# One Hymba decoder layer: the order of work inside a Mamba-2 chunk group, and the place of two small gate bounds

## The chip, the cores and the metric

The kernel runs on one core of one Trainium2 chip, as a single launch. The metric is the device time of a launch in microseconds (us); smaller is better. One core has a matrix engine (PE), a vector engine (DVE), a scalar engine (ACT), a general engine (POOL) and an engine that mostly issues transfers (SP). Each engine works through its own queue strictly in order, and semaphores make an instruction wait for work of another engine or for a transfer.

## The reference

One inference step of a hybrid decoder layer for a prompt of 1024 tokens (with 16 learned tokens ahead of it, so 1040) and 8 single-token samples, width 1024. In outline:

```python
h = h + 0.5 * swiglu(rmsnorm(h, n1), w1g, w1u, w1d)          # FFN1
u = rmsnorm(h, nm) @ w_in                                    # one input projection
# HGRN2 heads: lb comes from lb_logits alone
lb = cumsum(softmax(lb_logits, axis=0), axis=0)[layer]
f = lb + (1 - lb) * sigmoid(u_f) ...
# Mamba-2 heads, chunk by chunk (128 tokens):
def step(h, inp):
    xc, dtc, bc, cc = inp
    cum = cumsum(dtc * a_g, axis=1)
    seg = exp(where(causal, cum_t - cum_s, -inf))
    cb  = einsum('btgn,bsgn->bgts', cc, bc)
    y   = einsum('bgts,bgrts,bsgr,bsgrp->btgrp', cb, seg, dtc, xc)
    y   = y + einsum('btgn,bgrpn,btgr->btgrp', cc, h, exp(cum))
    h   = h * exp(last) + einsum('bsgn,bsgr,bgrpn...', bc, dtc * exp(last - cum), xc)
    return h, y
h = h + concat(hgrn_out, ssm_out) @ w_out
h = h + 0.5 * swiglu(rmsnorm(h, n2), w2g, w2u, w2d)          # FFN2
```

All inputs and outputs are f32.

## The kernel before, in words

The layer is written as one program: FFN1, the input projection, the Mamba-2 scan, the HGRN2 heads, the output projection, FFN2. Large products are made of three matmuls each, on operands split in a high and a low part (`mm3`, L173 to L175). The order of the instructions on PE is the order of the code; on the other engines a scheduler sets it when the program is built, from the code's order and its own due times, and it is fixed from then on.

The Mamba-2 scan (`ssm_scan`, L1610) runs over nine chunks c, eight of 128 tokens and one of 16. `front(c)` prepares a chunk, `back(c, hT)` makes its output and the next state. One **group** of the scan is `back(c)`, `front(c + 2)` and then `fill(10)`, ten steps of the input projections of later heads, of three matmuls each, which give PE work while the other engines prepare the next group. What the letters stand for:

- `mt`, the decay mask of a chunk for 8 heads (128 x 1024). SP issues its transfer (L1622, 512 KB, from `cumd`), ACT makes it with eight relu instructions (L1649) and one exp (L1650), and DVE multiplies it with `cbm`, the masked B-C products (L1644), in two instructions (L1652). It takes the buffer that the mask of chunk c-2 had.
- `xdt` (L1638), `xw` (L1653): the inputs scaled, on DVE, from `px`, a transpose on PE (L1633). `xw` is split: `xh` on ACT (L167), `xl` on DVE (L168).
- `bt`: the transposed B (PE L1641 into `pb`, where L1643 puts the B-C products too), its high part cast on ACT (L1645), its low part on DVE (L1646).
- `pi`: PE's product of state and C (L1667), read by DVE L1668. `py`: PE's product of `xdt` and `mt` (L1672), read by the add DVE L1675. Then four L1688 write the outputs.
- `ps`: PE's state product of `bt`, `xh`, `xl` (twelve matmuls on tiles `t`). The new state hn is the old one times a decay (DVE L1684) plus `ps` (DVE L1685). The next `pi` needs hn.

px, pb, pi, py and ps share four PSUM banks (tag `mis`) in rotation, in the order in which the code asks for them: in a group of the kernel before pi, py, ps, px, pb. So pb stands five places behind pi and gets the bank that pi had in the same group.

`constants_mix` (L1256) prepares small constants between FFN1 and the projections. Its seven small DVE instructions L1285 to L1294 and one ACT exp (L1288) make `lb` and `oml`, the bounds of the HGRN2 gates. `after1` places single steps into the second half of FFN1 by the number of a step (`S.before(e3 + ..., ...)`).

Of the kernel before, what the change touches and what calls it, by code (L numbers as in the profile page):

```python
# [2 lines left out]

# [14 lines left out]
P = 128  # L18
# [20 lines left out]
CT = [(128 * c, 128) for c in range(8)] + [(1024, 16)]  # L39
# [279 lines left out]
def new_x(K):  # L319
    K.xhi, K.xlo = ([K.slot("u", T, F32R) for k in range(KT)] for i in range(2))  # L320
# [932 lines left out]
    return lambda: columns(first, prm[:8, P : 2 * P]), lambda: columns(K.col, prm[: n - 8, :P])  # L1253


def constants_mix(K, a):  # L1256
    nc = K.nc
    cst = K.const

    K.st, K.st0 = K.pack(), K.pack("u")  # L1260

    K.tri = cst.tile([P, P], F32, name="tri")
    nc.gpsimd.affine_select(K.tri, K.ones[1], pattern=[[1, P]], compare_op=ALU.is_ge, fill=0.0, base=0, channel_multiplier=-1)

    K.mid = cst.tile([P, 32], U8, name="mid")
    for r in range(0, P, 32):
        nc.gpsimd.tensor_copy(K.mid[r : r + 32], K.ident[r : r + 32, r : r + 32])
    K.mask = {}
    for m in LEVELS[:5]:
        nb = 64 // m  # L1270
        f = K.sml.tile([P, 64], F32, tag="mf", name=K.uid("mf"))
        fv = f.rearrange("p (b i) -> p b i", i=m)
        on = K.ones[1][:, :64].rearrange("p (b i) -> p b i", i=m)

        nc.gpsimd.affine_select(fv, on, pattern=[[-2 * m, nb], [0, m]], compare_op=ALU.is_ge, fill=0.0, base=0, channel_multiplier=1)
        nc.gpsimd.affine_select(fv, fv, pattern=[[2 * m, nb], [0, m]], compare_op=ALU.is_ge, fill=0.0, base=m - 1, channel_multiplier=-1)
        u = cst.tile([P, 16], U8, name=f"mask{m}")
        for r in range(0, P, 32):
            nc.gpsimd.tensor_copy(u[r : r + 32], f[r : r + 32, r // 2 : r // 2 + 16])
        K.mask[m] = u  # L1280


    l0, l1 = K.pc["lb_logits"][:, 0:4], K.pc["lb_logits"][:, 4:8]
    e = K.st0.tile([P, 12])
    nc.vector.tensor_max(e[:, 8:12], l0, l1)  # L1285
    nc.vector.tensor_sub(e[:, 0:4], l0, e[:, 8:12])
    nc.vector.tensor_sub(e[:, 4:8], l1, e[:, 8:12])
    nc.scalar.activation(e[:, 0:8], e[:, 0:8], AF.Exp)  # L1288
    nc.vector.tensor_add(e[:, 8:12], e[:, 0:4], e[:, 4:8])
    nc.vector.reciprocal(e[:, 8:12], e[:, 8:12])  # L1290
    K.lb = cst.tile([P, 4], F32, name="lb")
    K.oml = cst.tile([P, 4], F32, name="oml")
    nc.vector.tensor_mul(K.lb, e[:, 0:4], e[:, 8:12])
    nc.vector.tensor_scalar(K.oml, K.lb, -1.0, 1.0, ALU.mult, ALU.add)  # L1294

    K.dtb = K.st.tile([P, 8])
    nc.sync.dma_start(K.dtb, a["dt_bias"].to_broadcast([P, 8]))
    K.an = K.st.tile([P, 8])
    nc.sync.dma_start(K.an, a["a_log"].to_broadcast([P, 8]))
    nc.scalar.activation(K.an, K.an, AF.Exp)  # L1300
    nc.vector.tensor_scalar_mul(K.an, K.an, -1.0)
    K.dcol = K.st.tile([P, 4])
    for hf in range(2):
        nc.sync.dma_start(K.dcol[64 * hf : 64 * hf + 64, :], a["d_skip"].rearrange("l (j f) -> f l j", f=2)[hf].to_broadcast([64, 4]))

    K.sel16 = cst.tile([16, 8], F32, name="sel16")
# [303 lines left out]
def ssm_scan(K, a, o, fill):  # L1610
    nc = K.nc
    hts = K.pack()
    hbuf = [hts.tile([P, 512]) for _ in range(2)]
    xs, B, C = K.xs[0:4], K.xs[4:6], K.xs[6:8]
    state = {}

    def front(c):

        t0, n = CT[c]
        r8 = slice(8 * c, 8 * c + 8)  # L1620
        mt = K.slot("s", w=1024).rearrange("p (h t) -> p h t", h=8)
        nc.sync.dma_start(mt[:, :, :n], K.cumd[r8, :n].partition_broadcast(P))  # L1622
        tk = K.pack()
        ec, cbm = tk.tile([P, 4, P]), tk.tile([P, 2, P])
        bt, xh, xl = K.tr(), K.tr(), K.tr()
        cs = slice(t0, t0 + n)
        if c > 0:

            for f in range(2):
                nc.sync.dma_start(ec[64 * f : 64 * f + 64, :, :n], K.cumd[8 * c + f : 8 * c + 8 : 2, :n].partition_broadcast(64))  # L1630
        px = K.psm()
        for j in range(4):
            nc.tensor.transpose(px[:n, j * P : (j + 1) * P], xs[j][:, cs], K.ident)  # L1633
        xx = K.slot("s", w=1024)
        xdt = xx[:, 0:512]
        xw = xx[:, 512:1024]
        pxv = px[:n].rearrange("p (h d) -> p h d", h=8)
        nc.vector.tensor_mul(xdt[:n].rearrange("p (h d) -> p h d", h=8), pxv, K.dt[:n, r8][:, :, None].broadcast_to([n, 8, 64]))  # L1638
        pb = K.psm()
        for g in range(2):  # L1640
            nc.tensor.transpose(pb[:n, g * P : (g + 1) * P], B[g][:, cs], K.ident)  # L1641
        for g in range(2):
            nc.tensor.matmul(pb[:n, 256 + g * P : 256 + g * P + n], B[g][:, cs], C[g][:, cs], start=True, stop=True)  # L1643
        nc.vector.tensor_mul(cbm[:n, :, :n], pb[:n, 256:512].rearrange("p (g t) -> p g t", g=2)[:, :, :n], K.tri[:n, None, :n].broadcast_to([n, 2, n]))  # L1644
        nc.scalar.copy(bt[:n, 0:256], pb[:n, 0:256])  # L1645
        nc.vector.tensor_sub(bt[:n, 256:512], pb[:n, 0:256], bt[:n, 0:256].bitcast(F32))  # L1646

        for hh in range(8):
            nc.scalar.activation(mt[:n, hh, :n], mt[:n, hh, :n], AF.Relu, scale=-1.0, bias=K.cum[:n, 8 * c + hh : 8 * c + hh + 1])  # L1649
        nc.scalar.activation(mt[:n, :, :n], mt[:n, :, :n], AF.Exp, scale=-1.0)  # L1650
        for g in range(2):
            nc.vector.tensor_mul(mt[:n, 4 * g : 4 * g + 4, :n], mt[:n, 4 * g : 4 * g + 4, :n], cbm[:n, g, None, :n].broadcast_to([n, 4, n]))  # L1652
        nc.vector.tensor_mul(xw[:n].rearrange("p (h d) -> p h d", h=8), pxv, K.wdec[:n, r8][:, :, None].broadcast_to([n, 8, 64]))  # L1653
        K.split(xw[:n], xh[:n], xl[:n])
        if c > 0:
            nc.scalar.activation(ec[:, :, :n], ec[:, :, :n], AF.Exp)
        state[c] = mt, ec, bt, xdt, xh, xl

    def back(c, hT):
        t0, n = CT[c]  # L1660
        r8 = slice(8 * c, 8 * c + 8)
        cs = slice(t0, t0 + n)
        mt, ec, bt, xdt, xh, xl = state.pop(c)
# [6 lines left out]
        for hh in range(8):  # L1670
            j, f = divmod(hh, 2)
            nc.tensor.matmul(py[64 * f : 64 * f + 64, j * P : j * P + n], xdt[:n, 64 * hh : 64 * hh + 64], mt[:n, hh, :n], start=True, stop=True)  # L1672
        pyv = py.rearrange("p (j t) -> p j t", j=4)
        if c > 0:
            nc.vector.tensor_add(ec[:, :, :n], pyv[:, :, :n], ec[:, :, :n])  # L1675
        ps = K.psm()
        for g in range(2):
            gs, xs_ = slice(g * P, g * P + P), slice(256 * g, 256 * g + 256)
            K.mm3(ps[:, xs_], bt[:n, gs], bt[:n, 256 + g * P : 256 + g * P + P], xh[:n, xs_], xl[:n, xs_], True, True)
        hn = hbuf[c % 2]  # L1680
        if c == 0:
            nc.scalar.copy(hn, ps)
        else:
            nc.vector.tensor_mul(hn.rearrange("p (h d) -> p h d", h=8), hT.rearrange("p (h d) -> p h d", h=8), K.ecl[:, r8][:, :, None].broadcast_to([P, 8, 64]))  # L1684
            nc.vector.tensor_add(hn, hn, ps)  # L1685
        for j in range(4):
            yj = ec[:, j, :n] if c > 0 else pyv[:, j, :n]
            nc.vector.scalar_tensor_tensor(xs[j][:, cs], xs[j][:, cs], K.dcol[:, j : j + 1], yj, ALU.mult, ALU.add)  # L1688
        return hn

    fill(14)
    front(0)
    fill(6)
    front(1)
    fill(10)
    hT = None
    for c in range(NC):
        hT = back(c, hT)
        if c + 2 < NC:
            front(c + 2)  # L1700
        if c + 1 == NC:
            sample_steps(K)
        fill(10 if c + 1 < NC else 6)
    pf = K.psm()
    for j in range(4):
# [7 lines left out]
def sample_steps(K):  # L1713

    nc = K.nc
    pd = K.psm()
    nc.tensor.transpose(pd[:8, 0:8], K.dt[:8, 72:80], K.ident[:8, :8])
    nc.tensor.transpose(pd[:8, 8:16], K.da[:8, 72:80], K.ident[:8, :8])
    K.dT = K.st.tile([8, 16])
    nc.vector.tensor_copy(K.dT, pd[:8, 0:16])  # L1720
# [518 lines left out]
def body(ctx, tc, a, o):  # L2239
# [95 lines left out]
    def after1(S, h, e3, e0, e1):  # L2335
# [17 lines left out]
        for q in (1, 3):  # L2353
            S.before(e3 + q + 7, lambda q=q: nm.begin(q))
            S.before(e3 + q + 9, lambda q=q: nm.finish(q))
        S.before(e0, lambda: new_x(K))
        S.before(e0 + 2, lambda: nm.end(0))
        S.before(e0 + 2, lambda: x_mix(0))
# [223 lines left out]
```

## Time and profile before

| | |
|---|---|
| times of three runs | 1930.01, 1928.18, 1926.17 us (median 1928.18) |
| profiled execution, its own time | 1926.92 us |
| its span, first to last instruction | 1925.1 us |
| mean granted clock of PE | 0.998 |
| busy: PE, PEld | 1906.6 us (99%), 1878.2 us (98%) |
| busy: DVE, ACT, POOL | 1535.1 us (80%), 860.6 us (45%), 32.6 us (2%) |
| groups of the scan | from about 820 to 900 us of the span |

The profiled execution is 1.26 us under the median of the three runs and has 1.82 us outside its span. PE waits for next to nothing, so the time is PE's work and the few places where PE stands still. A row of a timeline names start, duration, engine, line, operation, output and inputs; what stands in brackets is the idle time of the engine ahead of it and what ended it.

### The profile page before, as it was taken

The numbers are of one execution on the slowest core, as the hardware profiler recorded it, in microseconds if no ns is written. First come the engines' busy times: TensorE is split into PE (matmuls) and PEld (weight loads), VectorE is DVE, ScalarE is ACT, GpSimd is POOL, SyncE is SP. The second block draws the span as 40 slices with busy tenths as digits, with TensorE's granted clock in tenths as the row PEclk, the third lists the DMA queues.
The fourth block names the chain that finished last, engine by engine and source line by source line (L and its number), as shares of the span: only waits on it lengthen the run. The fifth ranks groups of instructions, "written<-read, shape, count | busy, mean of one in ns | idle before, by whom it ended". The sixth has DMA issues, their size and how long they took to land.

```text
span 1925.1 us, 41283 instructions
## 1 busy us (share of the span) xinstructions
PE 1906.6 (99%) x16726; PEld 1878.2 (98%) x16726; DVE 1535.1 (80%) x2887; ACT 860.6 (45%) x1634; POOL 32.6 (2%) x88
## 2 busy tenths in 40 slices
PE   9999999999999999999999999999999999999998
PEld 9999999999999999989999999999999999999998
DVE  7988888889789877677585567999888888978974
ACT  6533333334534654466564554743333333453353
POOL 3000000000000000000000000000000000000000
PEclk9999999999999999999999999999999999999999
DMA  8143333335967542221453254233323333586852
GB/s 249 55 122 95 95 106 111 95 95 179 305 219 232 168 149 56 62 87 32 118 175 99 69 177 146 59 113 113 100 89 102 102 111 94 170 267 210 274 182 87
DMA packets 324210, 258.48 MB, mean 134 GB/s; under 512 B 18923, under 2 KB 298731, under 8 KB 324011
## 3 DMA queue, kind: packets, MB, share of 16 engines
q1 hardware_dynamic: 323779, 255.79, 43.2%
q8 instruction: 132, 2.16, 0.5%
q14 instruction: 59, 0.48, 0.1%
q0 software_dynamic: 224, 0.04, 0.0%
q10 hardware_dynamic: 16, 0.00, 0.0%
HBM read 190.79 MB, written 65.05 MB: 133 GB/s over the span
## 4 chain that ended last, share of the span: by engine, by line
PE 95%; DVE 2%; ACT 1%; DMA 1%; issue 0%; SPq 0%; DVEq 0%; ACTq 0%
PE acc L173 24%; PE acc L175 24%; PE acc L174 24%; PE mis L173 6%; PE mis L175 6%; PE mis L174 6%; PE mis L1977 1%; DMA s<-cumd 1%; PE mis L2044 0%; DMA s<-in_x_prompt_dram 0%; PE mis L2069 0%; PE mis L1966 0%; PE mis L1672 0%; PE mis L2071 0%; PE mis L233 0%
## 5 line engine op out<-in xcount | busy, mean ns | idle before, releaser
L173 PE MATMUL acc<-u,ws 128*128 128x258 f32 (+4 forms) x3634 | 1064.2, 293 | 1.1 <-DVE u L1285 0.8
L175 PE MATMUL acc<-u,ws 128*128 128x258 f32 (+4 forms) x3634 | 1056.3, 291 | 0.6 <-DVE ws L505 0.6
L174 PE MATMUL acc<-u,ws 128*128 128x258 f32 (+4 forms) x3634 | 1054.5, 290 | 0.4 <-issue 0.4
L173 PEld LDWEIGHTS acc<-u,ws 128*128 128x128 f32 x3634 | 686.4, 189 | 8.6 <-issue 6.1
L174 PEld LDWEIGHTS acc<-u,ws 128*128 128x128 f32 x3634 | 687.8, 189 | 0.7 <-DVE u L334 0.2
L175 PEld LDWEIGHTS acc<-u,ws 128*128 128x128 f32 x3634 | 685.7, 189 | 2.1 <-DVE ws L505 1.1
L175 PE MATMUL mis<-u,ws 128*128 128x262 f32 (+1 forms) x810 | 229.8, 284 | 0.0
L173 PE MATMUL mis<-u,ws 128*128 128x262 f32 (+1 forms) x810 | 229.7, 284 | 0.0
L174 PE MATMUL mis<-u,ws 128*128 128x262 f32 (+1 forms) x738 | 208.5, 283 | 0.0
L505 DVE TENSOR_TENSOR ws<-r,ws 128x512 fp32r<-128x512 f32 x266 | 181.9, 685 | 4.4 <-ACT ws L501 4.2
L905 ACT ACTIVATE t<-t 128x524 f32<-128x524 f32 (+1 forms) x72 | 46.1, 640 | 299.9 <-DVE t L902 299.9
L501 ACT CAST ws<-r 128x512 fp32r<-128x512 f32 x266 | 156.8, 615 | 42.2 <-PE mis L175 18.0
L173 PEld LDWEIGHTS mis<-u,ws 128*128 128x128 f32 x810 | 153.3, 189 | 0.0
L175 PEld LDWEIGHTS mis<-u,ws 128*128 128x128 f32 x810 | 152.7, 188 | 0.0
L174 PEld LDWEIGHTS mis<-u,ws 128*128 128x128 f32 x738 | 139.8, 189 | 0.0
L497 DVE TENSOR_TENSOR r<-r,r 128x512 f32<-128x512 f32 x150 | 101.0, 685 | 0.2
L1035 DVE TENSOR_TENSOR u<-u,u 128x1048 fp32r<-128x1048 f32 (+3 forms) x84 | 96.1, 1146 | 4.9 <-ACT u L1031 4.9
L1093 ACT CAST ws<-u 128x512 fp32r<-128x512 f32 (+1 forms) x72 | 42.1, 585 | 109.6 <-DVE u L1088 104.9
L168 DVE TENSOR_TENSOR ws<-r,ws 128x512 fp32r<-128x512 f32 x88 | 59.5, 687 | 38.3 <-ACT ws L167 35.7
L1031 ACT CAST u<-u 128x1048 fp32r<-128x1048 f32 (+3 forms) x84 | 82.9, 989 | 1.4 <-DMA u<-hd 1.4
L1122 DVE SCALAR_TENSOR_TENSOR s<-acc,s 128x524 f32<-128x524 f32 (+3 forms) x86 | 54.0, 651 | 36.7 <-PE acc L175 36.3
L902 DVE TENSOR_TENSOR t<-t,u 128x524 f32<-128x524 f32 (+1 forms) x108 | 73.4, 693 | 0.1
(473 smaller groups left out, 2357.5 us busy)
## 6 DMA issues: line engine op xcount, KB each, us to landing
r<-in_w_ffn_down_dram SPq DMA_DIRECT2D x128, 256.0 KB
hd<-s SPq DMA_DIRECT2D x93, 258.0 KB
r<-in_w_ffn_gate_dram SPq DMA_DIRECT2D x88, 256.0 KB
r<-in_w_ffn_up_dram SPq DMA_DIRECT2D x88, 256.0 KB
hd<-s SPq DMA_DIRECT2D x77, 262.0 KB
u<-hd SPq DMA_DIRECT2D x36, 516.0 KB
u<-hd SPq DMA_DIRECT2D x28, 524.0 KB
r<-in_w_in_dram SPq DMA_DIRECT2D x56, 256.0 KB
```

Source lines behind the costliest of these rows:

```text
L168: self.nc.vector.tensor_sub(lo, src, hi.bitcast(F32))
L173: mm(ps, whi, xhi, start=first, stop=False, skip_group_check=more)
L174: mm(ps, whi, xlo, start=False, stop=False, skip_group_check=more)
L175: mm(ps, wlo, xhi, start=False, stop=last, skip_group_check=more)
L497: self.K.nc.vector.tensor_tensor(self.raw[p], self.raw[x], self.raw[y], op)
L501: self.K.nc.scalar.copy(self.w[p][:, : self.n * P], self.raw[p])
L505: self.K.nc.vector.tensor_sub(t[:, 512 : 512 + w], self.raw[p], t[:, :w].bitcast(F32))
L902: nc.vector.tensor_mul(t, t if src is None else src, spread.lanes(n, slice(0, 2)))
L905: nc.scalar.activation(t, t, AF.Silu)
L1031: K.nc.scalar.copy(hi, lo.bitcast(F32))
L1035: K.nc.vector.tensor_sub(lo, lo.bitcast(F32), hi.bitcast(F32))
L1122: nc.vector.scalar_tensor_tensor(t, b, 0.5, t, ALU.mult, ALU.add)
```

## The change

Three things are moved; no arithmetic is added or taken away.

1. The bounds: the code from L1285 to L1294 becomes a function `bounds(K)`, called from `after1` before step e3 - 20 of FFN1. Its small tile comes from another pool. One ACT table load more is in the program.
2. The masks: the two multiplies of `mt` with `cbm` and the subtraction that makes `xl` leave `front(c)` and stand in a function `rest()`. In the loop, `rest()` of chunk c+1 is called behind the output part of `back(c)`, and the scheduler is told to issue it after the add that reads `py`.
3. The state: `ps` and hn leave `back(c)` and become `carry(c)`, called after `front(c + 2)`, ahead of the fill. The banks are asked for in the order pi, py, px, pb, ps.

```diff
@@ front
-        for g in range(2):
-            nc.vector.tensor_mul(mt[...], mt[...], cbm[...])
         nc.vector.tensor_mul(xw[:n]..., pxv, K.wdec[...])
-        K.split(xw[:n], xh[:n], xl[:n])
+        nc.scalar.copy(xh[:n], xw[:n])
         if c > 0:
             nc.scalar.activation(ec[:, :, :n], ec[:, :, :n], AF.Exp)
+
+        def rest():
+            for g in range(2):
+                nc.vector.tensor_mul(mt[...], mt[...], cbm[...])
+            nc.vector.tensor_sub(xl[:n], xw[:n], xh[:n].bitcast(F32))
+
         state[c] = mt, ec, bt, xdt, xh, xl
+        rests[c] = rest
@@ back
         if c > 0:
-            nc.vector.tensor_add(ec[:, :, :n], pyv[:, :, :n], ec[:, :, :n])
+            an = nc.vector.tensor_add(ec[:, :, :n], pyv[:, :, :n], ec[:, :, :n])
+        for j in range(4):
+            ...
+        state[c] = bt, xh, xl
+        return an
+
+    def carry(c, hT):
+        ...
         ps = K.psm()
         for g in range(2):
             K.mm3(ps[...], bt[...], bt[...], xh[...], xl[...], True, True)
         hn = hbuf[c % 2]
         if c == 0:
             nc.scalar.copy(hn, ps)
         else:
             nc.vector.tensor_mul(hn..., hT..., K.ecl[...])
             nc.vector.tensor_add(hn, hn, ps)
-        for j in range(4):
-            ...
         return hn
@@ the loop
     fill(14)
     front(0)
     fill(6)
+    rests.pop(0)()
     front(1)
     fill(10)
     for c in range(NC):
-        hT = back(c, hT)
+        an = back(c, hT)
+        if c + 1 in rests:
+            with K.tc.issue_after(an.ins) if an else nullcontext():
+                rests.pop(c + 1)()
         if c + 2 < NC:
             front(c + 2)
         if c + 1 == NC:
             sample_steps(K)
+        hT = carry(c, hT)
         fill(10 if c + 1 < NC else 6)
@@ after1
+        S.before(e3 - 20, lambda: bounds(K))
```

In the changed kernel the lines have other numbers: px L1636, xdt L1641, pb L1644 and L1646, cbm L1647, the cast of bt L1648, its low part L1649, relu L1652, exp L1653, xw L1654, xh L1655, masks L1661, xl L1662, pi L1675 and its reader L1676, py L1680 and its reader L1684, the outputs L1687, the old state times its decay L1703, hn L1704. The bounds are L1260 to L1269.

On DVE in the group of chunk 1, before, from the reader of `pi` (L1668) on; `s_10042` is the tile of the outputs of chunk 1, `s_9917` the state, `s_10143` the mask of chunk 2, and tiles of chunk 3 are those of L1644, L1638 and L1646:

```order
L1668 TENSOR_TENSOR s_10042<-mis_10214,s_10042 128x512
L1675 TENSOR_TENSOR s_10042<-mis_10220,s_10042 128x512
L1685 TENSOR_TENSOR s_9917<-s_9917,mis_10230 128x512
L1652 TENSOR_TENSOR s_10143<-s_10143,s_10145 128x512 x2
L1688 SCALAR_TENSOR_TENSOR u_9198<-u_9198,s_8950,s_10042 128x128
L1688 SCALAR_TENSOR_TENSOR u_9235<-u_9235,s_8950,s_10042 128x128
L1688 SCALAR_TENSOR_TENSOR u_9272<-u_9272,s_8950,s_10042 128x128
L1688 SCALAR_TENSOR_TENSOR u_9487<-u_9487,s_8950,s_10042 128x128
L1644 TENSOR_TENSOR s_10245<-mis_10258,tri 128x256
L1638 TENSOR_TENSOR s_10256<-mis_10251,s_8950 128x512
L1646 TENSOR_TENSOR t_10246<-mis_10258,t_10246 128x256
```

On DVE in the same group, after; `s_10043` is the tile of the outputs, `s_10136` the mask of chunk 2, `t_10238` the split B of chunk 3, `s_9918` the state; `L1676` and `L1684` stand right ahead of these rows:

```order
L1661 TENSOR_TENSOR s_10136<-s_10136,s_10138 128x512
L1687 SCALAR_TENSOR_TENSOR u_9199<-u_9199,s_8950,s_10043 128x128
L1687 SCALAR_TENSOR_TENSOR u_9236<-u_9236,s_8950,s_10043 128x128
L1687 SCALAR_TENSOR_TENSOR u_9273<-u_9273,s_8950,s_10043 128x128
L1687 SCALAR_TENSOR_TENSOR u_9488<-u_9488,s_8950,s_10043 128x128
L1661 TENSOR_TENSOR s_10136<-s_10136,s_10138 128x512
L1662 TENSOR_TENSOR t_10141<-s_10149,t_10140 128x512
L1641 TENSOR_TENSOR s_10248<-mis_10243,s_8950 128x512
L1647 TENSOR_TENSOR s_10237<-mis_10250,tri 128x256
L1654 TENSOR_TENSOR s_10248<-mis_10243,s_8950 128x512
L1649 TENSOR_TENSOR t_10238<-mis_10250,t_10238 128x256
L1704 TENSOR_TENSOR s_9918<-s_9918,mis_10270 128x512
```

The add that makes the new state was the third of the group (L1685) and is now the last (L1704), behind the low part of `bt` of chunk 3 (L1649), which reads what ACT's cast L1648 of chunk 3 writes.

On ACT, before, the instructions on chunk 3 (its mask is `s_10243`, its split B `t_10246`):

```order
L1649 ACTIVATE s_10243<-s_10243,s_8950 128x128 x4
L1645 CAST t_10246<-mis_10258 128x256
L1649 ACTIVATE s_10243<-s_10243,s_8950 128x128 x4
L1656 ACTIVATE s_10245<-s_10245 128x512
L1650 ACTIVATE s_10243<-s_10243 128x1024
L167 CAST t_10247<-s_10256 128x512
```

On ACT, after, the same (the mask of chunk 3 is `s_10235`, its split B `t_10238`):

```order
L1652 ACTIVATE s_10235<-s_10235,s_8950 128x128 x5
L1648 CAST t_10238<-mis_10250 128x256
L1652 ACTIVATE s_10235<-s_10235,s_8950 128x128 x3
L1655 CAST t_10239<-s_10248 128x512
L1653 ACT_TABLE_LOAD
L1653 ACTIVATE s_10235<-s_10235 128x1024
```

The cast stands behind five of the eight relus of its chunk (four before). For chunk 5 the numbers are six and two. In the kernel before the casts of chunks 4 and 5 (L1645) stand ahead of all eight relus. For the last chunk, of 16 tokens, the cast stands in the kernel after behind its eight relus, its two exps and a copy L1876 of a finished projection (`acc`) out of PSUM; before, it stood ahead of that copy (there L1855).

On PE the twelve matmuls of `ps` move from behind `py` to behind `pb`; the count of instructions does not change.

More of the change, by code (lines that the diff above doesn't have):

```diff
@@ L1 @@
 import math
-from contextlib import ExitStack
+from contextlib import ExitStack, nullcontext
 import concourse.bass as bass
@@ L1253, in parameters, with bounds @@
     return lambda: columns(first, prm[:8, P : 2 * P]), lambda: columns(K.col, prm[: n - 8, :P])
+def bounds(K):
+    nc, cst = K.nc, K.const
+    l0, l1 = K.pc["lb_logits"][:, 0:4], K.pc["lb_logits"][:, 4:8]
+    e = K.sml.tile([P, 12], F32, tag="lbe", name="lbe", bufs=1)
+    nc.vector.tensor_max(e[:, 8:12], l0, l1)
+    nc.vector.tensor_sub(e[:, 0:4], l0, e[:, 8:12])
+    nc.vector.tensor_sub(e[:, 4:8], l1, e[:, 8:12])
+    nc.scalar.activation(e[:, 0:8], e[:, 0:8], AF.Exp)
+    nc.vector.tensor_add(e[:, 8:12], e[:, 0:4], e[:, 4:8])
+    nc.vector.reciprocal(e[:, 8:12], e[:, 8:12])
+    K.lb = cst.tile([P, 4], F32, name="lb")
+    K.oml = cst.tile([P, 4], F32, name="oml")
+    nc.vector.tensor_mul(K.lb, e[:, 0:4], e[:, 8:12])
+    nc.vector.tensor_scalar(K.oml, K.lb, -1.0, 1.0, ALU.mult, ALU.add)
 def constants_mix(K, a):
@@ L1280, in constants_mix @@
         K.mask[m] = u
[L1283 to L1294, printed above, removed]
     K.dtb = K.st.tile([P, 8])
@@ L1614, in ssm_scan @@
     xs, B, C = K.xs[0:4], K.xs[4:6], K.xs[6:8]
-    state = {}
+    state, rests = {}, {}
     def front(c):
@@ L1650, in front @@
         nc.scalar.activation(mt[:n, :, :n], mt[:n, :, :n], AF.Exp, scale=-1.0)
-        for g in range(2):
-            nc.vector.tensor_mul(mt[:n, 4 * g : 4 * g + 4, :n], mt[:n, 4 * g : 4 * g + 4, :n], cbm[:n, g, None, :n].broadcast_to([n, 4, n]))
         nc.vector.tensor_mul(xw[:n].rearrange("p (h d) -> p h d", h=8), pxv, K.wdec[:n, r8][:, :, None].broadcast_to([n, 8, 64]))
-        K.split(xw[:n], xh[:n], xl[:n])
+        nc.scalar.copy(xh[:n], xw[:n])
         if c > 0:
             nc.scalar.activation(ec[:, :, :n], ec[:, :, :n], AF.Exp)
+        def rest():
+            for g in range(2):
+                nc.vector.tensor_mul(mt[:n, 4 * g : 4 * g + 4, :n], mt[:n, 4 * g : 4 * g + 4, :n], cbm[:n, g, None, :n].broadcast_to([n, 4, n]))
+            nc.vector.tensor_sub(xl[:n], xw[:n], xh[:n].bitcast(F32))
         state[c] = mt, ec, bt, xdt, xh, xl
+        rests[c] = rest
     def back(c, hT):
@@ L1673, in back @@
         pyv = py.rearrange("p (j t) -> p j t", j=4)
+        an = None
         if c > 0:
-            nc.vector.tensor_add(ec[:, :, :n], pyv[:, :, :n], ec[:, :, :n])
+            an = nc.vector.tensor_add(ec[:, :, :n], pyv[:, :, :n], ec[:, :, :n])
+        for j in range(4):
+            yj = ec[:, j, :n] if c > 0 else pyv[:, j, :n]
+            nc.vector.scalar_tensor_tensor(xs[j][:, cs], xs[j][:, cs], K.dcol[:, j : j + 1], yj, ALU.mult, ALU.add)
+        state[c] = bt, xh, xl
+        return an
+    def carry(c, hT):
+        n = CT[c][1]
+        r8 = slice(8 * c, 8 * c + 8)
+        bt, xh, xl = state.pop(c)
         ps = K.psm()
         for g in range(2):
-            gs, xs_ = slice(g * P, g * P + P), slice(256 * g, 256 * g + 256)
-            K.mm3(ps[:, xs_], bt[:n, gs], bt[:n, 256 + g * P : 256 + g * P + P], xh[:n, xs_], xl[:n, xs_], True, True)
+            gs, xg = slice(g * P, g * P + P), slice(256 * g, 256 * g + 256)
+            K.mm3(ps[:, xg], bt[:n, gs], bt[:n, 256 + g * P : 256 + g * P + P], xh[:n, xg], xl[:n, xg], True, True)
         hn = hbuf[c % 2]
@@ L1685, in back @@
             nc.vector.tensor_add(hn, hn, ps)
-        for j in range(4):
-            yj = ec[:, j, :n] if c > 0 else pyv[:, j, :n]
-            nc.vector.scalar_tensor_tensor(xs[j][:, cs], xs[j][:, cs], K.dcol[:, j : j + 1], yj, ALU.mult, ALU.add)
         return hn
```

## The prediction

> **What bounds the kernel now.** I began with the first part of the page, the busy times.
>
> ```profile
> span 1925.1 us, 41283 instructions
> PE 1906.6 (99%) x16726; PEld 1878.2 (98%) x16726; DVE 1535.1 (80%) x2887; ACT 860.6 (45%) x1634; POOL 32.6 (2%) x88
> ```
>
> PE is busy for all but 18.5 us. The change takes no matmul away, so it can only win where PE stands still or runs at a lower clock. The second view is the list of PE's waits, by line and by the line that ended them.
>
> ```profile
> PE mis L1641 <- DVE s L1668: 4.1, 2, 2.5
> ...
> PE acc L173 <- DVE u L1285: 0.8, 1, 0.8
> ```
>
> The largest is in the scan: `pb` (L1641) waited twice, 4.1 us in all, for DVE's read of `pi` (L1668), whose bank it takes over. The second row shown names a bound (L1285). The rest of the list belongs to work that isn't touched. The third view is the timeline of both stalls, on PE and on DVE.
>
> ```profile
> 844.78 0.44 PE L1641 MATMUL mis<-ident,u 128*128 128x128 f32 x2 [2.45 <-DVE s L1668]
> ...
> 865.62 0.44 PE L1641 MATMUL mis<-ident,u 128*128 128x128 f32 x2 [1.60 <-DVE s L1668]
> ```
>
> ```profile
> 842.23 1.29 DVE L1652 TENSOR_TENSOR s<-s,s 128x512 f32<-128x512 f32 x2 [1.03 <-ACT s L1650]
> 843.44 0.68 DVE L168 TENSOR_TENSOR t<-s,t 128x512 fp32r<-128x512 f32 x1
> 844.04 0.68 DVE L1668 TENSOR_TENSOR s<-mis,s 128x512 f32<-128x512 f32 x1
> ...
> 846.16 1.13 DVE L1688 SCALAR_TENSOR_TENSOR u<-u,s,s 128x128 f32<-128x128 f32 x4
> ...
> 863.06 1.29 DVE L1652 TENSOR_TENSOR s<-s,s 128x512 f32<-128x512 f32 x2 [3.40 <-ACT s L1650]
> ```
>
> L1668 could have run as soon as `pi` was done, but it stands in DVE's queue behind the masks L1652 of the next chunk, which waited for ACT's exp. In the chain of waits I looked for what ACT waited for.
>
> ```profile
> 831.24 1.05 PE mis L1672 x16
> 832.34 5.58 DMA s<-cumd
> ...
> 854.01 5.08 DMA s<-cumd
> ```
>
> So both stalls start with a transfer of a mask that landed 5.58 and 5.08 us after its issue. In the chain it follows on `py` (L1672): it takes the buffer that `py` has just read, so SP issues it when `py` ends. The rest of this chain matters for the new order as well. It is read on ACT, then on DVE, and the third fence shows the next `pi` on PE.
>
> ```profile
> 838.01 1.28 ACT L1649 ACTIVATE s<-s,s 128x128 f32<-128x128 f32 x4 [3.75 <-DMA s<-cumd]
> 839.20 0.34 ACT L1645 CAST t<-mis 128x256 fp32r<-128x256 f32 x1
> ...
> 859.11 2.45 ACT L1649 ACTIVATE s<-s,s 128x128 f32<-128x128 f32 x8 [2.21 <-DMA s<-cumd]
> ```
>
> ```profile
> 839.58 0.42 DVE L1646 TENSOR_TENSOR t<-mis,t 128x256 fp32r<-128x256 f32 x1 [2.49 <-ACT t L1645]
> 839.92 0.68 DVE L1653 TENSOR_TENSOR s<-mis,s 128x512 f32<-128x512 f32 x1
> ```
>
> ```profile
> 838.91 1.05 PE L1667 MATMUL mis<-u,s 128*128 128x128 f32 x8
> ...
> 860.57 1.05 PE L1667 MATMUL mis<-u,s 128*128 128x128 f32 x8
> ```
>
> The last view is a table of windows, for the clock after each stall; its columns end with the granted clock, the DMA share and GB/s.
>
> ```profile
> 860.00:880.00 20.00, 18.39 (x148) 17.58 (x147) 16.27 (x33) 17.02 (x40) 0.00 (x0) 1.00 0.24 79
> 845.00:846.00 1.00, 1.00 (x9) 1.00 (x8) 1.00 (x3) 0.00 (x0) 0.00 (x0) 0.87 0.11 33
> 846.00:848.00 2.00, 2.00 (x9) 2.00 (x8) 2.00 (x7) 1.72 (x6) 0.00 (x0) 0.50 0.00 0
> 848.00:850.00 2.00, 2.00 (x11) 2.00 (x10) 2.00 (x5) 2.00 (x6) 0.00 (x0) 0.71 0.00 0
> ```
>
> After the gap of 2.45 us PE was granted less clock for some 4 us: the loss is 0.13 + 2 x 0.50 + 2 x 0.29 = 1.71 us. After the gap of 1.60 us the clock stayed at 1.00. All that the scan's two stalls cost is therefore 2.45 + 1.60 + 1.71 = 5.76 us.
>
> [...]
>
> **The change, part by part.** *The old wait goes.* With L1676 (the read of `pi`) ahead of the masks, the bank of `pi` is free about 0.7 us after `pi` ends, one 128x512 instruction. The masks of the next chunk then stand behind the reads of `py`, a whole group after their transfer. `pb` is now fourth behind `pi` and takes the bank of the preceding `ps`, which hn has read before `pi` could start. So neither of the two old waits has a cause left: -4.05 us, and -1.71 us if no new gap replaces the first.
>
> *A new wait comes.* The next `pi` needs hn. In the kernel before, hn (L1685) stood early in DVE's queue. Now L1704 is the last of the group, and right ahead of it stands L1649, the low part of `bt` of chunk c+2. That needs ACT's cast L1648, which ACT has put behind five or six relus of the same chunk, and these wait for the mask's transfer, the one that is issued at the end of `py`. The new path of each group is: end of `py`, landing, five relus, cast, L1649, L1704, next `pi`. Queued behind the waiting L1649 are hn and the whole next group of DVE; PE waits at `pi` as soon as its fill is used up.
>
> The price, from rows. Four relus took 1.19 us (838.01 to 839.20), 0.30 each. From the start of the cast to that of DVE's low part are 0.38 us (839.20 to 839.58), to the next DVE instruction 0.34 (to 839.92), and from the start of a 128x512 on DVE to the PE work that waits for it 0.74 (844.04 to 844.78): together 1.46 us. With the landing of 5.58 us, relus from 838.01: 838.01 + 1.49 + 1.46 = 840.96, where `pi` started at 838.91. New gap 2.05 us. With the landing of 5.08 us and six relus: 859.11 + 1.79 + 1.46 = 862.36 against 860.57, new gap 1.79 us.
>
> For the landings of the other groups the only rows are bounds: SP's issues, and when ACT began on that mask.
>
> ```profile
> 873.22 0.33 SPq L1622 DMA_DIRECT2D s<-cumd  x1
> ```
>
> ```profile
> 876.99 2.44 ACT L1649 ACTIVATE s<-s,s 128x128 f32<-128x128 f32 x8
> ```
>
> Here the landing took at most 3.77 us. From the end of `py` to the next `pi` PE needs 838.91 - 832.34 = 6.57 us. So the gap is the landing + 1.49 + 1.46 - 6.57, or landing minus 3.62: at most 0.15 us here, and nothing in a group that lands earlier. I take 0.15 once. DVE alone does not hold hn up. Behind `py` it has the add, `xl`, `xdt` and `xw` (0.60 each, 843.44 to 844.04), masks 1.21 (842.23 to 843.44), outputs 1.13, `cbm` 0.42 and L1649 0.34 as the rows of L1646 show them, then 0.74: 6.24 us, a third of a microsecond under 6.57.
>
> In the last group but two the cast of the short chunk, which was ahead of a copy out of PSUM, is put behind it.
>
> ```profile
> 887.17 0.36 ACT L1645 CAST t<-mis 16x256 fp32r<-16x256 f32 x1
> 887.44 0.43 ACT L1855 COPY u<-acc 128x344 f32<-128x344 f32 x1
> 887.77 0.61 ACT L167 CAST ws<-r 128x512 fp32r<-128x512 f32 x1
> ```
>
> ```profile
> 888.32 1.05 PE L1667 MATMUL mis<-u,s 128*128 128x128 f32 x8
> ```
>
> If the copy runs where it did, the cast starts at 887.77, and `pi` at 887.77 + 1.46 = 889.23 instead of 888.32: a gap of 0.91 us. If the copy could run 0.27 earlier, 0.64. I take 0.9.
>
> Sum of new gaps: 2.05 + 1.79 + 0.15 + 0.9 = 4.89 us, against 4.05 removed. The gap of 2.05 us lies between one that dropped the clock and one that did not. I count one drop of 1.71 us in the changed kernel, as before; the bounds are none and two. The other moves have one answer: `ps` behind `pb` is the same PE work, and the masks and `xl` are the same DVE work; a table load that now stands ahead of the exp of chunk 3 is covered, since its masks are wanted only after the next `py`.
>
> *The bounds.* In FFN1 DVE gets seven small instructions and ACT an exp with a table load ahead of it.
>
> ```profile
> L1290 DVE RECIPROCAL u<-u 128x4 f32<-128x4 f32 x1 | 0.2, 178 | 0.0
> L1650 ACT ACT_TABLE_LOAD x4 | 5.1, 1283 | 0.1
> ```
>
> ```profile
> 611.75 0.69 DVE L1098 TENSOR_TENSOR ws<-u,ws 128x512 fp32r<-128x512 f32 x1 [0.76 <-ACT ws L1093]
> ...
> 621.27 0.70 DVE L1122 SCALAR_TENSOR_TENSOR s<-acc,s 128x524 f32<-128x524 f32 x1
> ```
>
> ```profile
> 605.00:625.00 20.00, 20.00 (x166) 20.00 (x166) 17.55 (x30) 8.58 (x17) 0.00 (x0) 1.00 0.82 264
> ```
>
> Seven times up to 0.18 and a wait for ACT's table load (1.28) and exp (I take 0.2 as for DVE's small ones) are some 2.7 us on DVE, ahead of the weight part made at 611.75. PE uses that part only in the accumulation that follows the one read out at 621.27, and DVE is idle for 2.45 of the 20 us of this window. Cost 0; were that cover gone, up to 2.7 us. What goes at 700 us:
>
> ```profile
> 700.27 0.59 PE L173 MATMUL acc<-u,ws 128*128 128x350 f32 x2 [0.77 <-DVE u L1285]
> ```
>
> ```profile
> 699.29 0.89 DVE L331 SCALAR_TENSOR_TENSOR t<-s,col,t 128x262 f32<-128x262 f32 x2
> 700.09 0.16 DVE L1285 TENSOR_TENSOR u<-col 128x4 f32<-128x4 f32 x1
> ```
>
> The row names L1285, but that instruction is no input of the matmul; DVE was making the normed input (L331) until 700.1, so the wait stays when L1285 goes. The bounds of the gain are 0 and 0.77 us; I take 0.1.
>
> **Sum.** -4.05 - 1.71 + 4.89 + 1.71 - 0.1 = +0.74 us, on the profiled execution of 1926.92 us (its span of 1925.1 and 1.82 around it): 1927.66. That execution lies 1.26 us under the median of the three runs, so on the scale of the median it is 1928.9 us against 1928.18. The three runs lie 3.84 us apart, 0.2% of the time, and I call nothing smaller a difference.
>
> **The rivals.** *The full gain.* The two late landings may be a chance of that execution, or the shifted groups may avoid them. With landings up to 3.77 us only the gap of the short chunk is left: -5.76 + 0.15 + 0.9 - 0.1 = -4.81 us, or 1923.4. For it: PE's list has only two such waits, so the other groups' landings did no harm. Against it: nothing in the change touches what the transfer does or when in the group it starts.
>
> *Slower: late landings are now paid in more places.* In the old order a late mask held a read of `pi` and a bank; now it holds the state itself, in every group, with all over 3.62 us paid. With a third landing of 5.08 us and two drops of the clock: 2.05 + 2 x 1.79 + 0.9 + 2 x 1.71 = 9.95, less 5.76 and 0.1, is +4.1 us, or 1932.3. It decides from the third late landing on, or from 4.3 us in each of the five other groups. For it: gaps of about 2 us lie near the one that cost clock. Against it: the rows show two late landings, not three.
>
> *The clock holds.* All as in the forecast, with no drop after the gap of 2.05 us: +0.74 - 1.71 = -0.97 us, or 1927.2. [...] The only gap of over 2 us in these rows says otherwise.
>
> *The change does nothing where it counts*: the forecast in another form, since the transfer's landing, and not the masks' place in the queue, sets the length of the late groups.
>
> **How the numbers follow.** The forecast 0.30, the clock holds 0.18, the full gain 0.25, slower 0.24, anything else 0.03. The full gain gives most of faster by over 0.2% (0.24); forecast, clock and the near edge of the gain are within 0.2% (0.51); the rest is slower (0.25). The likeliest case's own range, with 0 to 2 drops of the clock and the bounds of the small terms, is 1926 to 1931. The full range, with a tenth left out at each end, is 1922.8 (the full gain, the short chunk's gap gone in part) to 1933.0 (a little over the priced slower case).
>
> **What would show it.** Right: PE's waits no longer list pb behind the reader of `pi`; instead `pi` (L1675) waits for DVE L1704, two or three times, with some 2 us as the longest, and in these groups DVE's L1649 waits for ACT L1648. Wrong: no wait at L1675 (then the landings were short: the full gain), or waits there in most groups (slower); a wait of PE near 612 us would refute the cover of the bounds.

## The result, and the profile after

| | before | after |
|---|---|---|
| median of nine runs each | 1928.45 us (1926.17 to 1930.21) | 1923.17 us (1920.78 to 1925.5) |
| profiled execution: time, span | 1926.92, 1925.1 us | 1922.44, 1920.7 us |
| granted clock of PE | 0.998 | 0.999 |

The ratio is 0.9974, with a 95% interval of 0.9964 to 0.9984: 3 to 7 us faster, some 5 us in the middle. The forecast was 1928.9 us, no difference, with a fourth of the chance on faster. The busy times of the changed kernel:

```profile
span 1920.7 us, 41288 instructions
PE 1904.0 (99%) x16726; PEld 1874.1 (98%) x16726; DVE 1535.9 (80%) x2887; ACT 861.3 (45%) x1635; POOL 30.4 (2%) x88
```

The span is 4.4 us shorter, and PE's busy time 2.6 us: more than half of the difference is not idle time of PE at all. The lowered clock of the profile before, which stretches busy matmuls by some 1.71 us, is one part of these 2.6 us. PE's waits:

```profile
PE mis L1675 <- DVE s L1704: 3.2, 5, 1.7
...
PE acc L173 <- ACT u L332: 0.8, 1, 0.8
```

Both waits of `pb` are gone, and a new one stands at `pi` for hn, five times. The wait at 700 us stays at 0.8 us; with the bound gone the profile names the cast of the normed input (L332). The five new waits on PE's timeline, and the chain of waits around the longest, which shows landing, relus, cast, low part and the state's add in this order:

```profile
839.13 0.71 PE L1675 MATMUL mis<-u,s 128*128 128x128 f32 x4 [0.71 <-DVE s L1704]
848.25 0.60 PE L1675 MATMUL mis<-u,s 128*128 128x128 f32 x3 [0.15 <-DVE s L1704]
858.85 0.60 PE L1675 MATMUL mis<-u,s 128*128 128x128 f32 x3 [1.72 <-DVE s L1704]
876.47 0.60 PE L1675 MATMUL mis<-u,s 128*128 128x128 f32 x3 [0.16 <-DVE s L1704]
885.74 0.49 PE L1675 MATMUL mis<-u,s 128*128 128x128 f32 x2 [0.50 <-DVE s L1704]
```

```profile
831.78 4.34 DMA s<-cumd
...
841.39 3.84 DMA s<-cumd
...
850.51 5.03 DMA s<-cumd
855.62 0.19 ACT s L1652
855.93 1.55 ACT s L1652 x5
857.49 0.27 ACT t L1648
857.77 0.42 DVE t L1649
858.20 0.61 DVE s L1704
858.85 1.16 PE mis L1675 x8
...
869.72 3.74 DMA s<-cumd
```

The windows of the scan show no lowered clock:

```profile
840.00:860.00 20.00, 18.12 (x145) 16.86 (x145) 15.97 (x32) 13.10 (x31) 0.00 (x0) 1.00 0.26 80
860.00:880.00 20.00, 19.84 (x171) 18.48 (x171) 18.78 (x37) 17.03 (x37) 0.00 (x0) 1.00 0.27 80
```

So the scan did what the prediction described, at lower prices for the new waits. But the time also went away where the change touches no instruction. A fixed stretch of FFN2, from ACT's cast L760 to the one read of a `mis` bank by DVE's L1122, shows it. Before, then after (timelines of ACT and DVE):

```profile
1317.00 0.63 ACT L760 CAST s<-s 128x516 fp32r<-128x516 f32 x1 [3.29 <-DVE s L752]
...
1883.39 0.42 DVE L1122 SCALAR_TENSOR_TENSOR s<-mis,s 128x258 f32<-128x258 f32 x1
```

```profile
1313.92 0.62 ACT L760 CAST s<-s 128x516 fp32r<-128x516 f32 x1 [3.31 <-DVE s L752]
...
1879.04 0.42 DVE L1122 SCALAR_TENSOR_TENSOR s<-mis,s 128x258 f32<-128x258 f32 x1
```

It took 566.39 us before and takes 565.12 us after, 1.27 us less in work that is the same. The groups of instructions by shape say which: FFN2's matmuls on `u`. Before, then after:

```profile
L173 PE MATMUL acc<-u,ws 128*128 128x258 f32 x1601 | 454.0, 284 | 0.2 <-DVE t L609 0.2
L175 PE MATMUL acc<-u,ws 128*128 128x258 f32 x1601 | 453.0, 283 | 0.2 <-DVE ws L505 0.2
```

```profile
L173 PE MATMUL acc<-u,ws 128*128 128x258 f32 x1601 | 453.4, 283 | 0.2 <-DVE t L609 0.2
L175 PE MATMUL acc<-u,ws 128*128 128x258 f32 x1601 | 451.8, 282 | 0.2 <-DVE ws L505 0.2
```

What differs for these matmuls between the two programs is their addresses. The bounds' tile of 48 bytes per partition is new in the pool of small tiles, and the pool of the large tiles (`s` and `u`) lies behind it: in the built program its first tile moves from byte 67968 of a partition to 68032, 64 bytes up. The small tiles behind the new one move by 64 bytes too; `ws`, the other operand of these matmuls, lies in a pool ahead of them and stays.

### The profile page after: what moved, and what is told of

Its sections match the earlier page's. It is cut to its first block, busy times and chain, and to the rows that moved or that the text cites. A ratio compares the mean times of both kernels' runs of the same rounds, so it can differ in the third digit from the quotient of the medians.

```text
span 1920.7 us, 41288 instructions
## 1 busy us (share of the span) xinstructions
PE 1904.0 (99%) x16726; PEld 1874.1 (98%) x16726; DVE 1535.9 (80%) x2887; ACT 861.3 (45%) x1635; POOL 30.4 (2%) x88
## 4 chain that ended last, share of the span: by engine, by line
PE 94%; DVE 2%; ACT 2%; DMA 1%; issue 0%; DVEq 0%; SPq 0%; ACTq 0%
PE acc L173 24%; PE acc L175 24%; PE acc L174 24%; PE mis L173 6%; PE mis L174 6%; PE mis L175 6%; DMA s<-cumd 1%; PE mis L1998 1%; PE mis L2065 0%; ACT s L1652 0%; PE mis L1680 0%; PE mis L1675 0%; PE mis L2090 0%; PE mis L1987 0%; PE mis L2092 0%
## 5 line engine op out<-in xcount | busy, mean ns | idle before, releaser
L173 PE MATMUL acc<-u,ws 128*128 128x258 f32 (+4 forms) x3634 | 1061.7, 292 | 1.0 <-ACT u L332 0.8
L175 PE MATMUL acc<-u,ws 128*128 128x258 f32 (+4 forms) x3634 | 1054.3, 290 | 0.9 <-DVE ws L505 0.9
L173 PEld LDWEIGHTS acc<-u,ws 128*128 128x128 f32 x3634 | 684.7, 188 | 8.5 <-issue 6.1
L175 PEld LDWEIGHTS acc<-u,ws 128*128 128x128 f32 x3634 | 686.1, 189 | 2.4 <-DVE ws L505 1.5
L173 PE MATMUL mis<-u,ws 128*128 128x262 f32 (+1 forms) x810 | 230.1, 284 | 0.0
L175 PE MATMUL mis<-u,ws 128*128 128x262 f32 (+1 forms) x810 | 229.2, 283 | 0.0
L173 PEld LDWEIGHTS mis<-u,ws 128*128 128x128 f32 x810 | 153.0, 189 | 0.0
L175 PEld LDWEIGHTS mis<-u,ws 128*128 128x128 f32 x810 | 152.9, 189 | 0.0
L1122 DVE SCALAR_TENSOR_TENSOR s<-acc,s 128x524 f32<-128x524 f32 (+3 forms) x86 | 53.9, 650 | 33.6 <-PE acc L175 33.3
L819 ACT CAST ws<-t 128x512 fp32r<-128x512 f32 (+1 forms) x54 | 29.6, 548 | 98.0 <-DVE t L808 57.0
```

The source lines that it names most:

```text
L173: mm(ps, whi, xhi, start=first, stop=False, skip_group_check=more)
L175: mm(ps, wlo, xhi, start=False, stop=last, skip_group_check=more)
L1122: nc.vector.scalar_tensor_tensor(t, b, 0.5, t, ALU.mult, ALU.add)
```

## The experiments

**The two parts of the change, each alone.** The theory then was that the whole gain comes from the scan; the rival, that moving the bounds is worth something of its own. The first kernel is before with this edit:

```diff
-    (the bounds in constants_mix)
+        S.before(e3 - 20, lambda: bounds(K))
```

> The kernel before with the bounds alone moved into FFN1; the scan is untouched. Scan theory (the whole gain comes from the waits of the scan): no change, within 1 us of the kernel before, and PE still waits twice at pb (L1641) for the read of pi, with the clock lowered after the longer gap. Rival, the bounds are worth something of their own (the gap of 0.8 us at 700 us, or a shifted second half): faster by 1 to 2.5 us with both waits at pb still there.

Measured: ratio 0.9987 (0.9978 to 0.9997), some 2.5 us, with medians of 1925.62 and 1926.86 us. Its profile still waits at `pb`:

```profile
PE mis L1644 <- DVE s L1671: 2.3, 1, 2.3
```

The second is the changed kernel with the opposite edit, the scan alone:

> The changed kernel with the bounds put back behind FFN1. Scan theory: as the changed kernel, 4 to 5.5 us faster than before; PE's list has no wait at pb, and some 3 us at pi (L1675) behind the state's add. Rival, the bounds carry part of it: only 2 to 3.5 us faster than before.

Measured: ratio 0.9992 (0.9983 to 1.0), median 1926.43 against 1926.86 us. Its `pi` waits 2.2 us in three pieces of up to 1.3 us, in the place that the theory names, but the gain is 1.5 us by the ratio where 4 to 5.5 were expected:

```profile
PE mis L1672 <- DVE s L1701: 2.2, 3, 1.3
```

Its stretch of FFN2 takes 566.47 us (1316.18 to 1882.65), that of before. The scan theory falls: neither part is the whole of the gain, and their shares, 2.5 and 1.5 us, can't be told apart within these intervals. The one wait that names a bound, at 700 us, stays when the bounds are moved, so I looked for their share in the addresses.

**The addresses alone.** To the kernel before an unused tile is added, which leaves every engine's instructions as they are, but for addresses:

```diff
     K.mask = {}
+    K.sml.tile([P, 12], F32, tag="pad", name="pad", bufs=1)
```

> The kernel before with an unused tile of 48 bytes per partition in the pool of small tiles, which moves every large tile (the slots u and s, that the matmuls read) up by 64 bytes, as the tile of the moved bounds does; every engine's instructions are those of before. Layout theory (the bounds gain by where their tile puts the others, not by their time): 1 to 2.5 us faster than before, as the kernel with the bounds alone; the same instruction of the second FFN falls back against before by some 1.3 us between 1020 and 1880 us. Rival, the bounds gain by being out of the way behind FFN1, or the difference was chance: no change, within 0.8 us, and no drift.

Measured: ratio 0.9984 (0.9975 to 0.9993), median 1924.22 against 1927.29 us. Its stretch of FFN2 takes 564.53 us, and the same groups are shorter:

```profile
1315.52 0.62 ACT L760 CAST s<-s 128x516 fp32r<-128x516 f32 x1 [3.31 <-DVE s L752]
...
1880.05 0.42 DVE L1122 SCALAR_TENSOR_TENSOR s<-mis,s 128x258 f32<-128x258 f32 x1
```

```profile
L173 PE MATMUL acc<-u,ws 128*128 128x258 f32 x1601 | 453.2, 283 | 0.2 <-DVE t L609 0.2
...
L175 PE MATMUL acc<-u,ws 128*128 128x258 f32 x1601 | 451.5, 282 | 0.2 <-DVE ws L505 0.2
```

This kernel has the old waits at `pb` (3.2 us) and the lowered clock after them (0.66 from 845 to 850 us, as before), and its instructions are those of before, so its gain goes with the 64 bytes by which the large tiles moved. The rival falls. Of the 3 us that the ratio makes, 1.86 are seen in this stretch of FFN2 and 0.82 in the corresponding one of FFN1 (from the first cast L760 to the one read of a `mis` bank: 573.18 us before, 572.36 here). The granted clocks listed with the runs, 0.9974 in the mean of these 11 and 0.9970 of before's 23, could by an estimate make 0.8 us of the difference, since a thousandth of the time is 1.9 us. Two more sizes, a tile of 112 bytes (`[P, 28]`) and one of 32 bytes (`[P, 8]`):

> As the padded kernel, with a tile of 112 bytes, which moves the large tiles up by 128 bytes. If what counts is the address modulo 128: no change against before, no drift in the second FFN. If any other move gives the same drift, 1 to 2.5 us faster.

> The kernel before with an unused tile of 32 bytes, which moves the large tiles by 32 bytes. If any place off the multiple of 128 is as good: 2 to 4 us faster than before, the 128x258 groups at 453.2 and 451.5 us. If it is the place modulo 64 that counts: another value, faster or slower, that cannot be said beforehand; no change if only 64 helps.

Measured: 128 bytes, ratio 0.9996 (0.9987 to 1.0004), FFN2's stretch 566.51 us, no change. 32 bytes, ratio 0.9987 (0.9978 to 0.9996), but the 128x258 groups of L173 and L175 at 454.8 and 452.6 us are no faster than before as a whole; the stretch of FFN2 takes 565.9 us. FFN1 doesn't follow FFN2: its stretch takes 572.35 us with 128 bytes and 571.51 with 32, against 573.18 before, so most of what the 32 bytes gain lies there. So 64 bytes took 1.86 us off FFN2's stretch and 0.82 off FFN1's, 32 bytes 0.49 and 1.67, and 128 bytes nothing off FFN2's and 0.83 off FFN1's, in one execution each; that the place modulo 128 decides is not shown, and a rule for other sizes does not follow from these runs.

**The change without the move.** The changed kernel with 64 bytes more, which brings the large tiles to 128 bytes above their place of before:

```diff
     K.mask = {}
+    K.sml.tile([P, 16], F32, tag="pad", name="pad", bufs=1)
```

> The changed kernel with an unused tile of 64 bytes more, so that the large tiles stand where they stood before, modulo 128 bytes; all instructions are those of the changed kernel. Theory (about 3 us of the gain is the move by 64 bytes, the rest the scan): 1 to 3 us faster than before, 2 to 4 us slower than the changed kernel; the groups of 128x258 matmuls on u take 454.0, 453.0 and 452 us as before. Rival, the bounds behind FFN1 cost something that the change saves: 4 to 5.5 us faster than before, as the changed kernel.

Measured: ratio 0.9993 (0.9984 to 1.0002), median 1925.07 against 1927.24 us; FFN2's stretch 566.62 us (1314.87 to 1881.49), and the 128x258 groups 453.9, 453.6 and 452.4 us. The instructions of the change, bounds and scan, are worth 1.3 us, within noise of nothing; the rest of the gain goes with the 64 bytes. The clocks listed with the runs (mean 0.9980, and 0.9971 for before's 21) would by the same estimate make 1.7 us: what is left of the gain can all be a lowered clock that comes less often. The rival (the bounds' work behind FFN1 cost something) falls.

**The halves of the scan's change.** In the first kernel the masks go behind the reads, and state product and hn stay behind `py`; in the second the state goes last, and the masks stay in `front`. Both have the bounds, and so the 64 bytes.

```diff
 (masks only)
-    def carry(c, hT): ...
+    (its body stays in back(), behind the add that reads py)
-        hT = carry(c, hT)
```

> The masks and xl behind the reads of the preceding chunk, as in the change, but the state product and the state's add where they were (behind py), and the bounds moved. Theory (what made the old gaps is the masks' place in DVE's queue; what made the new ones is the late add of the state): no wait at pb and none of over 0.3 us at pi, no lowered clock in the scan, 1 to 3 us faster than the changed kernel, 5.5 to 8 us faster than before. Rival, the state product must go last for the bank of pi to come free: waits at pb come back, 1 to 2 us each, and it is no faster than the changed kernel.

Measured: ratio 0.9963 (0.9951 to 0.9975), 1920.19 against 1926.86 us, and no wait of the scan in PE's list. The clock did fall once in the scan, at 894 us (0.92 from 890 to 895 us, 0.73 from 895 to 900), where PE did not stand still; that part of the theory missed. The rival falls: with the read of `pi` ahead of the masks no wait at `pb` is listed, though the state product stays behind `py`.

```diff
 (state only)
-            nc.vector.tensor_mul(mt ...)          # in rest(), with xl
+            nc.vector.tensor_mul(mt ...)          # in front(), with xl, as before
```

> The changed kernel with the masks and xl back in front, so that the state product and the state's add go last but the masks stand ahead of the reads of the preceding chunk where the scheduler wants it so (bounds moved). Theory: pb no longer waits for pi's bank, but the read of pi and hn wait behind the masks or the cast in the groups with late landings, so PE waits at pi or py for 2 to 5 us in all; 0 to 3 us faster than before, no faster than the changed kernel. Rival, the state product's place is the whole of the gain: as fast as the changed kernel with waits of under 2 us.

Measured: ratio 0.9971 (0.9960 to 0.9983), 1922.5 us, one wait of 0.8 us. It is as fast as the changed kernel, as the rival has it, so my theory (2 to 5 us of waits) was wrong here. In this program ACT's casts of chunks 3 and 5 stand ahead of all relus and that of chunk 4 behind one; hn does not hang on the late landings. Either half alone removes the old waits; only both together, in the scheduler's order for them, put hn behind the landing.

**The new wait taken away.** The changed kernel with ACT's relus ordered behind the cast of their chunk:

```diff
-        nc.scalar.copy(bt[:n, 0:256], pb[:n, 0:256])
+        cp = nc.scalar.copy(bt[:n, 0:256], pb[:n, 0:256])
...
+        with K.tc.issue_after(cp.ins):
             for hh in range(8):
                 nc.scalar.activation(mt ..., AF.Relu, ...)
```

> The changed kernel, with ACT's relus of a chunk ordered behind its cast of bt, so that the state's add does not stand behind the landing of a mask. Theory of the new wait (landing, relus, cast, low part, add): the 3.2 us at pi fall under 0.6 us and the time by 2 to 3 us against the changed kernel. Rival, DVE's own queue behind py is as long as the group: waits at pi of 0.3 to 0.6 us stay in most groups and the time does not change.

Measured: ratio 0.9959 (0.9947 to 0.9971), 1919.88 us. PE's list has no wait of the scan left, where 3.2 us stood: the chain from the landing to hn is what PE waited for. It has the lowest ratio of the study, by the ratios some 3 us under the changed kernel's, though the two intervals overlap. The same edit on the kernel with the masks alone:

> The kernel with the masks behind the reads and the state's add early, with the relus ordered behind the cast of bt as well, and the bounds moved (large tiles moved by 64 bytes): neither the bank of pi nor the state hangs on a landing. Theory: no wait in the scan over 0.3 us, 6.5 to 8.5 us faster than before, level with or up to 1 us faster than the kernel with the cast first. Rival, the order of ACT around the last chunk costs something: a wait of 0.5 to 1 us at the last pi and no gain over the kernel with the cast first.

Measured: ratio 0.9967 (0.9954 to 0.9980), 1921.7 us, no wait of the scan either. The rival's wait at the last `pi` did not come; the gain is 6.4 us by the ratio, just under what was expected. The intervals of these two and of the masks alone overlap.

**What a gap costs in clock.** The kernel with the cast first, where the multiply of the old state with its decay is made again two, three and five times before hn of chunks 1, 3 and 5 (all these multiplies are ordered behind the add that reads `py`):

```diff
+                for _ in range(1 + {1: 2, 3: 3, 5: 5}.get(c, 0)):
                     nc.vector.tensor_mul(hn ..., hT ..., K.ecl ...)
```

> The kernel with the cast first, with the state's decay multiply made again 2, 3 and 5 times (same result) ahead of the state's add of chunks 1, 3 and 5, which holds pi up by about 1.5, 2 and 3.3 us. Theory A, the length of a gap sets the clock: no drop after the first, half clock for 3.4 us after the last, and the one between decides where. [...]

Measured: 1937.35 us, one execution. Gaps on PE's timeline, and windows with their granted clock as third number from the end:

```profile
842.04 1.13 PE L1676 MATMUL mis<-u,s 128*128 128x128 f32 x8 [2.12 <-DVE s L1707]
863.63 2.08 PE L1676 MATMUL mis<-u,s 128*128 128x128 f32 x8 [2.38 <-DVE s L1707]
874.76 1.13 PE L1676 MATMUL mis<-u,s 128*128 128x128 f32 x8 [0.69 <-DVE s L1707]
888.60 2.08 PE L1676 MATMUL mis<-u,s 128*128 128x128 f32 x8 [5.01 <-DVE s L1707]
```

```profile
845.00:850.00 5.00, 5.00 (x34) 5.00 (x33) 4.88 (x11) 1.39 (x5) 0.00 (x0) 0.85 0.47 157
865.00:870.00 5.00, 5.00 (x42) 4.61 (x41) 3.34 (x9) 0.00 (x0) 0.00 (x0) 0.80 0.29 95
875.00:880.00 5.00, 5.00 (x49) 4.71 (x49) 3.73 (x9) 4.94 (x7) 0.00 (x0) 1.00 0.35 124
890.00:895.00 5.00, 5.00 (x37) 3.68 (x36) 3.07 (x8) 0.00 (x0) 0.00 (x0) 0.57 0.12 12
```

Each of the three gaps over 2 us was followed by a lowered clock (0.85, 0.80 and 0.57 in the rows above), the one of 0.69 was not (1.00). In the other profiles a gap of 2.07 us (32 bytes) and one of 2.38 us (64 bytes) were followed by one (0.66 from 845 to 850 us in both), and one of 2.28 us (the bounds alone) was not; none of the scan's gaps up to 1.72 us was. And the scan-only kernel lost clock twice with PE busy for all 5.00 us of the window, after ten matmuls of 16x8 at 744 us and in the group of the short chunk:

```profile
745.00:750.00 5.00, 5.00 (x29) 4.70 (x29) 3.46 (x14) 1.95 (x4) 0.00 (x0) 0.72 0.62 159
...
895.00:900.00 5.00, 5.00 (x40) 4.84 (x40) 4.31 (x13) 0.45 (x1) 0.00 (x0) 0.74 0.00 0
```

The length of a gap alone doesn't decide, then. Before, the window with the gap of 2.45 us was followed by 3.41 us at a clock of 0.50; with the bounds alone, the clock stayed at 1.00 around the gap of 2.28 us, which ended at 843.88:

```profile
842.32:845.74 3.42, 0.97 (x9) 0.96 (x9) 3.42 (x6) 1.76 (x4) 0.00 (x0) 1.00 0.66 216
845.74:849.15 3.41, 3.41 (x14) 3.41 (x13) 3.41 (x10) 2.87 (x10) 0.00 (x0) 0.50 0.00 0
849.15:852.56 3.41, 3.41 (x25) 3.41 (x24) 3.28 (x6) 2.18 (x4) 0.00 (x0) 1.00 0.00 0
```

```profile
841.00:843.00 2.00, 0.60 (x6) 0.36 (x4) 1.67 (x3) 2.00 (x5) 0.00 (x0) 1.00 0.76 239
843.00:845.00 2.00, 1.12 (x9) 1.12 (x10) 2.00 (x5) 0.18 (x1) 0.00 (x0) 1.00 0.51 154
845.00:847.00 2.00, 2.00 (x14) 2.00 (x13) 2.00 (x8) 1.61 (x6) 0.00 (x0) 1.00 0.00 0
847.00:849.00 2.00, 2.00 (x15) 2.00 (x14) 2.00 (x4) 2.00 (x6) 0.00 (x0) 1.00 0.00 0
```

Summed over such windows (the length of each times what its clock lacks of 1.00), every lowered stretch named here cost 1.70 to 1.75 us, and the one after the gap of 5.01 us 3.45. What decides whether a gap costs clock, the runs do not show; none moved a gap on purpose to test it.

## Why the prediction was wrong

- **The step that failed is the price of the bounds.** "Cost 0", and a gain of 0.1 us at 700 us, are about right for their instructions: the wait at 700 us is still 0.8 us, and PE does not wait near 612 us. The diff says that the tile moves to another pool, and I costed its time, not its place. The tile moves what the matmuls read. In the padded kernel this alone is worth 0.16% (0.07% to 0.25%), about 3 us by the run times; with the large tiles 128 bytes above their place of before, 1.3 us are left of the change's 5. In the changed kernel's own profile 1.55 us of it are seen, in the two FFNs.
- **The old waits and their causes: right in place, from one execution in size.** Both went, as described. The profiles of four more kernels with the scan of before have 2.3, 3.2, 2.1 and 3.1 us at `pb` where 4.05 were taken, and two of the four have the lowered clock (64 and 32 bytes, 0.66 from 845 to 850 us). That wait is about as much as the new waits take (3.24 us, 2.2 in the scan alone, 1.8 in the change without the move), so the scan's reordering could gain little beyond the clock.
- **The new wait: right in place and chain, too dear in size.** The sum of 4.89 us measured 3.24. The rule "landing minus 3.62" gives 0.72, 0.22 and 0.12 us for the landings of 4.34, 3.84 and 3.74 us; measured were 0.71, 0.15 and 0.16. For the landing of 5.03 us with six relus (0.30 more) it gives 1.71, and 1.72 were measured. So the step that missed is the landing taken for chunk 3, 5.58 us from one execution, where 4.34 came. The wait of the short chunk was priced at 0.9 and came to 0.50 us.
- **The drop of the clock: the price was right, the count not.** I charged one drop for the gap of 2.05 us, by its length. No gap came over 1.72 us, and no drop. That is 1.71 us of the difference between the two profiles. Length does not order the gaps of the other runs: 2.07 us (32 bytes) and 2.12 us (the multiplies made again) were followed by a lowered clock, 0.66 from 845 to 850 us and 0.81 from 840 to 845, and 2.28 us (the bounds alone) was not, 1.00.
- **The rivals.** The full gain's number, 1923.4 us, was met to 0.2 us by a kernel that does not do what that rival says: it has 3.2 us of new waits and a landing of 5.03 us. That the number fits is luck: the 64 bytes, for which that sum has no term, stand in for waits that did not go. For the scan alone, the forecast's +0.84 us stands against -1.3 us (-3.1 to +0.4) for the change without the move: nearer to the forecast than to the full gain.

Of the 4.4 us between the two spans, 1.55 us lie in the two FFNs at the new addresses (1.27 us in the stretch of FFN2, and 0.28 in the corresponding one of FFN1, 573.18 to 572.90 us), 1.71 in the clock and 0.81 in waits of the scan (4.05 to 3.24). The remaining 0.3 us I do not place; the time up to FFN1's stretch is 0.24 us longer than before, so some 0.5 us were gained between the two FFNs outside these terms.

## What to carry to other kernels

PE is busy for 99% of this kernel's span, and the price of the change included what it did to PE's operands: a new tile of 48 bytes in one pool moved all that is allocated behind it, and some 0.4 and 0.75 ns a matmul in two groups of 1601 (1.55 us in the two FFNs' stretches) outweighed the 0.81 us of mended stalls. Test it with an unused tile before crediting a reordering with a gain. And when work that hung on a transfer is moved, follow the scheduled queues to the end: a step that must wait should stand behind the others on its engine, as the relus behind the cast here, which took 3.2 us of waits away.

## What the runs showed of the hardware

FFN2's stretch, the same work in every program, took 566.39, 566.47, 566.51 and 566.62 us in four programs with the large tiles at their old place or 128 bytes on (before, scan only, 128 bytes, change without the move), and 564.53 us in the padded program and 565.06 to 565.48 us in seven with the bounds moved, all eight with the large tiles 64 bytes on. Within the four it repeats to 0.23 us, closer than whole runs of one kernel agree (4 us). Each is one execution, and why they differ the runs do not say.

The transfer of the mask of chunk 3, 512 KB, landed after 5.58, 5.31, 5.48, 4.59 and 5.21 us in five programs with the scan of before (before, bounds only, 64, 128 and 32 bytes), and after 4.34, 4.95 and 3.94 us in three with the new one (changed, scan only, change without the move), in the same place of the program. A chain that hangs on it should be priced with that spread and not with one value.
